# Attention of a two-layer trunk: keys' remainder and meta values on all 128 rows, one tile for the meta probabilities, 24 gate steps ahead

## The chip, the cores and the metric

The kernel runs on one core of one Trainium2 chip. The metric is the device time of one execution in microseconds (us); lower is better. The core's engines work side by side: TensorE (PE in the profile, its weight loads PEld) for matmuls and transposes, VectorE (DVE), ScalarE (ACT), GpSimd (POOL), and SyncE (SP), which issues most DMAs. Each engine takes its own instructions in one fixed order.

## The reference, cut to what matters

The whole program is a two-layer trunk over 1040 tokens (16 meta tokens in front of 1024) of width 1024. The change touches layer 0's mixer, which has a recurrent part and an attention part side by side:

```
x_rnn, gate, q, k, v = split(h @ w_in)
y_rnn = gelu(gate) * rg_lru(x_rnn)            # conv, two sigmoid gates, a scan over time
q, k  = rotary(rmsnorm(q)), rotary(rmsnorm(k))   # 8 heads on 2 kv heads, 64 wide
# query blocks of 128 tokens; each sees 16 meta keys and 256 window keys
s = concat([q @ k_meta.T, q @ k_win.T]) * 64**-0.5, masked
p = softmax(concat([s, sink]))[..., :-1]
o = p[..., :16] @ v_meta + p[..., 16:] @ v_win
h = h + concat([y_rnn, o]) @ w_out
```

Behind it come a feed-forward layer, multi-scale retention and a second feed-forward layer, whose code the change leaves as it is. All is in float32.

## The kernel before, in words

**Precision.** A float32 operand of a large product is split into a rounded part "hi" and a remainder "lo" (`part`, L108; L111 and L113), and a product is three matmuls, hi·hi, lo·hi and hi·lo (`mm3`, L160 to L162). A scheduler puts the instructions of each engine into their order when the program is built; the code's order is its priority, and its own model of durations decides the rest.

**Before attention.** `rnn_in` makes the recurrent inputs, then four recurrences `recur(m)` (L387) and three groups of q/k/v projections are interleaved: keys and values first (grp 2), then two groups of queries. A recurrence goes over all engines in turn: matmuls and sigmoids (L403, L404), exp and tanh on ScalarE (L406, L407), L410 on VectorE, a square root on ScalarE (L411), products on GpSimd, and two scans on VectorE (L419). `qk_transpose` (L515) turns keys and queries into columns. Heads of kv group g lie on rows 64g to 64g+63. For the keys it writes `kH[g]`, the rounded keys of group g, on its own 64 rows (ScalarE) and once more on the other 64 (GpSimd, L525), and the remainder into `kTl`, where each group has only its own 64 rows (L526).

**Gates.** `gate_in(m)` (L434), m from 0 to 3, is the gate's projection: three chunks of 264, 264 and 512 columns, each 24 matmuls in 4 steps of 6, a product on VectorE and a GELU. For m = 0 that is one ScalarE function; for the others `gelu_tanh` (L424) computes it with two ScalarE passes (L427, L430), three VectorE passes (L428, L431, L432) and one on GpSimd (L429). Its work tile `u` lies in the pool `bp`. That pool takes over the memory of the recurrences' pool `la` (L565, L566), so its tiles wait for the last scan of `recur(3)`; the query tiles `q0` and `q1` lie there too. 12 steps (all of gate 0) are taken ahead of attention (L568); the rest is handed to `background()`, which runs one step after each score of a head.

**Attention.** Nine query blocks (the first of 16 rows), each in two steps, one for a kv group with its four heads; 18 steps. `queries` splits the block's queries: hi on the group's own 64 rows, lo on the other 64 (L624, L625). `scores` (L628) makes for each head a pair of matmuls into one bank: L636 with all 128 rows against `kH` (hi·hi + lo·hi) and L637 with 64 rows against `kTl` (hi·lo); then a masked minimum on VectorE (L639) and an exp on ScalarE (L641). GpSimd copies the 16 meta columns of the four heads into `pm` (L645). One step later, `transposes` turns the probabilities (L653) and `pm` (L658, 64 columns) and copies them to SBUF. Two steps later, `values` multiplies the meta part by `vmb[g]`, a 64-row matrix with the meta values of the four heads in block form (L666, 256 columns), and the window part head by head (L670). `finish` transposes the result (L687). After step 13 the first half of the output projection `out_proj(m, 0)` joins the background work; `gate_out` splits the gated recurrences at steps 10 to 13.

```
for _ in range(12):
    next(gates)
...
for i in range(ns + 4):
    ...
        scores(*steps[i])
    ...
        transposes(*steps[i - 1])
    ...
        values(*steps[i - 2])
```

## Time and profile before

| | us |
|---|---|
| median of 3 runs | 2723.39 |
| lowest and highest | 2717.32, 2725.48 |
| the profiled execution | 2719.58 |
| its span, first to last instruction | 2717.5 |
| TensorE busy in the span | 2639.5 |
| VectorE busy | 1650.9 |
| GpSimd busy | 1305.2 |
| ScalarE busy | 1131.8 |

A matmul's busy time in the profile includes its way through the array, so that busy times of neighbours overlap; what a matmul costs in a stream is the distance from its start to the next one's start. "Clock" is the share of the 2.4 GHz that was granted to TensorE; 0.50 is the lower of its two levels, 1.2 GHz. A bracket at a row's end gives the engine's idle time before it and what ended it.

### The profile page before, as it was taken

The numbers are of one execution on the slowest core, as the hardware profiler recorded it, in microseconds if no ns is written. First come the engines' busy times: TensorE is split into PE (matmuls) and PEld (weight loads), VectorE is DVE, ScalarE is ACT, GpSimd is POOL, SyncE is SP. The second block draws the span as 40 slices with busy tenths as digits, with TensorE's granted clock in tenths as the row PEclk, the third lists the DMA queues.
The fourth block names the chain that finished last, engine by engine and source line by source line (L and its number), as shares of the span: only waits on it lengthen the run. The fifth ranks groups of instructions, "written<-read, shape, count | busy, mean of one in ns | idle before, by whom it ended". The sixth has DMA issues, their size and how long they took to land.

```text
span 2717.5 us, 43025 instructions
## 1 busy us (share of the span) xinstructions
PE 2639.5 (97%) x16151; PEld 2331.9 (86%) x16151; DVE 1650.9 (61%) x2976; ACT 1131.8 (42%) x2328; POOL 1305.2 (48%) x1215
## 2 busy tenths in 40 slices
PE   8979999999999899999999999999998999998999
PEld 7867899999999899888888888888886788886777
DVE  6866675866666877634434454344378555556875
ACT  4665543433333433343434444334443333334442
POOL 3654233555545777533334243342444555565784
PEclk9989999999999999999999999999999999999999
DMA  4000142232232743222121242222241232226442
GB/s 150 26 30 16 64 152 83 102 110 87 98 111 99 266 137 95 102 77 78 57 92 63 85 137 74 86 78 73 84 140 62 93 113 97 102 89 233 160 150 89
DMA packets 111073, 274.60 MB, mean 101 GB/s; under 512 B 13520, under 2 KB 13776, under 8 KB 110864
## 3 DMA queue, kind: packets, MB, share of 16 engines
q1 hardware_dynamic: 87840, 228.86, 25.1%
q10 hardware_dynamic: 22464, 41.14, 4.0%
q8 instruction: 127, 2.08, 0.3%
q0 software_dynamic: 560, 1.85, 0.2%
q14 instruction: 82, 0.67, 0.1%
HBM read 216.37 MB, written 55.43 MB: 100 GB/s over the span
## 4 chain that ended last, share of the span: by engine, by line
PE 53%; DVE 3%; POOL 1%; ACT 1%; issue 1%; DMA 0%; SPq 0%; DVEq 0%; ACTq 0%; POOLq 0%
PE ps L161 13%; PE ps L160 13%; PE ps L162 13%; PE ax L160 4%; PE ax L161 4%; PE ax L162 4%; DVE lo L113 1%; PE ax L1081 1%; PE ax L186 1%; DVE xp L760 1%; PE ax L1135 0%; POOL ol L781 0%; DVE ol L781 0%; DVE T L775 0%; PE ax L1096 0%
## 5 line engine op out<-in xcount | busy, mean ns | idle before, releaser
L160 PE MATMUL ps<-oh,hi 128*128 128x260 f32 (+1 forms) x1584 | 506.2, 322 | 19.4 <-ACT oh L780 13.8
L162 PE MATMUL ps<-oh,lo 128*128 128x260 f32 (+1 forms) x1584 | 506.7, 321 | 10.5 <-DVE lo L113 10.4
L161 PE MATMUL ps<-ol,hi 128*128 128x260 f32 (+1 forms) x1584 | 508.7, 322 | 1.1 <-DVE ol L781 1.0
L111 ACT CAST hi<-raw 128x512 fp32r<-128x512 f32 (+2 forms) x476 | 284.6, 602 | 531.4 <-PE ps L161 345.8
L160 PE MATMUL ax<-oh,hi 128*128 128x260 f32 (+1 forms) x1212 | 388.0, 322 | 2.0 <-ACT hi L111 0.8
L162 PE MATMUL ax<-oh,lo 128*128 128x260 f32 (+1 forms) x1212 | 387.0, 321 | 2.6 <-DVE lo L113 2.6
L161 PE MATMUL ax<-ol,hi 128*128 128x260 f32 (+1 forms) x1212 | 389.0, 321 | 0.4 <-DVE ol L781 0.4
L113 DVE TENSOR_TENSOR lo<-raw,hi 128x512 fp32r<-128x512 f32 (+2 forms) x348 | 282.1, 813 | 113.8 <-ACT hi L111 103.8
L113 DVE TENSOR_TENSOR lo<-S,hi 128x512 fp32r<-128x512 f32 (+2 forms) x288 | 257.3, 896 | 138.3 <-ACT hi L111 132.5
L111 ACT CAST hi<-S 128x512 fp32r<-128x512 f32 (+2 forms) x288 | 161.2, 562 | 427.8 <-PE ps L161 186.8
L160 PEld LDWEIGHTS ps<-oh,hi 128*128 128x128 f32 x1584 | 298.4, 189 | 45.9 <-ACT oh L780 15.3
L162 PEld LDWEIGHTS ps<-oh,lo 128*128 128x128 f32 x1584 | 299.1, 189 | 36.7 <-DVE lo L113 13.3
L161 PEld LDWEIGHTS ps<-ol,hi 128*128 128x128 f32 x1584 | 299.2, 189 | 26.9 <-DVE ol L781 3.2
L113 POOL TENSOR_TENSOR lo<-raw,hi 128x512 fp32r<-128x512 f32 x128 | 166.0, 1304 | 266.9 <-ACT hi L111 255.6
L160 PE MATMUL ps<-xh,hi 128*128 128x512 f32 (+1 forms) x752 | 278.7, 372 | 10.7 <-ACT hi L111 7.1
L161 PE MATMUL ps<-xl,hi 128*128 128x512 f32 (+1 forms) x752 | 275.7, 367 | 1.7 <-DVE xl L210 1.1
L162 PE MATMUL ps<-xh,lo 128*128 128x512 f32 (+1 forms) x752 | 273.2, 364 | 0.0
L291 POOL TENSOR_TENSOR t<-t,rf 128x520 f32<-128x520 f32 (+1 forms) x148 | 215.3, 1464 | 78.8 <-DVE t L822 31.7
L160 PEld LDWEIGHTS ax<-oh,hi 128*128 128x128 f32 x1212 | 229.7, 190 | 21.4 <-ACT hi L111 1.2
L162 PEld LDWEIGHTS ax<-oh,lo 128*128 128x128 f32 x1212 | 229.2, 189 | 21.4 <-DVE lo L113 3.3
L161 PEld LDWEIGHTS ax<-ol,hi 128*128 128x128 f32 x1212 | 229.6, 189 | 19.0 <-DVE ol L781 0.8
L781 POOL TENSOR_TENSOR ol<-raw,oh 128x520 fp32r<-128x520 f32 (+1 forms) x140 | 204.9, 1491 | 26.0 <-ACT oh L780 13.1
(323 smaller groups left out, 5722.3 us busy)
## 6 DMA issues: line engine op xcount, KB each, us to landing
raw<-in_wr_dram SPq DMA_DIRECT2D x64, 512.0 KB, 3.2
raw<-in_wgu_dram SPq DMA_DIRECT2D x48, 512.0 KB, 3.3
rb<-in_wgu_dram SPq DMA_DIRECT2D x40, 512.0 KB, 3.2
raw<-hd SPq DMA_DIRECT2D x77, 260.0 KB, 3.8
raw<-hd SPq DMA_DIRECT2D x77, 256.0 KB, 3.0
raw<-in_wrv_dram SPq DMA_DIRECT2D x32, 512.0 KB, 3.2
raw<-in_wro_dram SPq DMA_DIRECT2D x32, 512.0 KB, 3.2
hd<-T ACTq DMA_DIRECT2D x44, 260.0 KB, 2.6
```

Source lines behind the costliest of these rows:

```text
L111: nc.scalar.copy(hi, src)
L113: eng.tensor_tensor(out=lo, in0=src, in1=f32(hi), op=ALU.subtract)
L160: nc.tensor.matmul(ps, ah, bh, start=first and i == 0, stop=False, skip_group_check=more)
L161: nc.tensor.matmul(ps, ah, bl, start=False, stop=False, skip_group_check=more)
L162: nc.tensor.matmul(ps, al, bh, start=False, stop=last and i == n - 1, skip_group_check=more)
L186: nc.tensor.matmul(o, a, b, start=first and i == 0 and j == 0, stop=end and j == 1)
L291: (eng or nc.vector).tensor_tensor(out=out_, in0=a, in1=b, op=ALU.mult)
L760: nc.vector.scalar_tensor_tensor(out=t[:, :n], in0=h[m][hf][:, :n], scalar=par(gname, m), in1=sc, op0=ALU.mult, op1=ALU.mult)
L781: eng.tensor_tensor(out=lo, in0=src, in1=f32(hi), op=ALU.subtract)
L1081: nc.tensor.matmul(ps[:, :P], kf[d][:, c:c + P], qf[d][:, c:c + P], start=d == 0, stop=d == 1)
```

## The change

- `kTl` becomes two tiles `kL[g]` with the remainder on all 128 rows: VectorE writes the group's own 64 rows as before, and GpSimd copies them to the other 64 (18 new copies). The second matmul of a score pair then takes all 128 rows of the query tile. On the added rows the query's lo meets the key's lo, a product that was left out before.
- The meta probabilities of both kv groups share one tile `pm` of 128 columns; it is transposed once per block, and the meta values are one 128-row matrix `vmb` of 512 columns, so that a block has one such matmul instead of two. `values` runs once per block, for all eight heads, when the second group's step is due.
- 24 gate steps, gates 0 and 1, are taken ahead of attention instead of 12, and `gelu_tanh`'s work tile comes from the general pool of slots instead of `bp`.
- For room: `part` with a pool gets one buffer instead of two, the first half of a weight unit uses the common pool, and `sn` has two buffers instead of three.

```diff
         def gelu_tanh(y, x, n):
-            u = bp.tile([P, 528], F32, tag="gu", bufs=1, name=nm("gu"))[:, :n]
+            u = slot("gu")[:, :n]
             nc.scalar.activation(u, x, AF.Square)
             nc.vector.scalar_tensor_tensor(out=u, in0=u, scalar=0.044715, in1=x, op0=ALU.mult, op1=ALU.mult)
             nc.gpsimd.tensor_tensor(out=u, in0=u, in1=x, op=ALU.add)
...
                     gs = slice(g * 64, (g + 1) * 64)
                     nc.scalar.copy(kH[g][(gs,) + at], src[gs])
                     nc.gpsimd.tensor_copy(kH[g][(slice(64 - g * 64, 128 - g * 64),) + at], kH[g][(gs,) + at])
-                    nc.vector.tensor_tensor(out=kTl[(gs,) + at], in0=src[gs], in1=f32(kH[g][(gs,) + at]),
+                    nc.vector.tensor_tensor(out=kL[g][(gs,) + at], in0=src[gs], in1=f32(kH[g][(gs,) + at]),
                                             op=ALU.subtract)
+                    nc.gpsimd.tensor_copy(kL[g][(slice(64 - g * 64, 128 - g * 64),) + at], kL[g][(gs,) + at])
             else:
                 for j in range(2):
                     nc.tensor.transpose(pt[:, j * P:j * P + n], qs[:n, j * P:(j + 1) * P], ident[:n, :n])
...
         lctx.close()
         bp = bctx.enter_context(tc.tile_pool(name="bp", bufs=1))
         gates = chain.from_iterable(gate_in(m) for m in range(4))
-        for _ in range(12):
+        for _ in range(24):
             next(gates)
         work = [gates]
...
         nsk = mp.tile([P, 8], F32, name="nsk")
         nc.vector.tensor_scalar(nsk, par("sink", 0, 8), -1.0, None, op0=ALU.mult)
-        vmb = []
+        vmb = mp.tile([P, 512], F32, name="vmb")
+        nc.gpsimd.memset(vmb, 0.0)
+        ps = bank()
+        nc.tensor.matmul(ps[:, :P], c0t[:NM, C0["rep"]:C0["rep"] + P], vt[:NM, 0, :], start=True, stop=True)
         for g in range(2):
-            ps = bank()
-            nc.tensor.matmul(ps[:64, :64], c0t[:NM, C0["rep"]:C0["rep"] + 64], vt[:NM, 0, g * 64:(g + 1) * 64],
-                             start=True, stop=True)
-            v_ = mp.tile([64, 256], F32, name=f"vmb{g}")
-            mul(v_.rearrange("p (h d) -> p h d", d=64), ps[:64, :64].unsqueeze(1).to_broadcast([64, 4, 64]),
-                c0t[:64, C0["bm"]:C0["bm"] + 256].rearrange("p (h d) -> p h d", d=64))
-            vmb.append(v_)
+            gs = slice(g * 64, (g + 1) * 64)
+            mul(vmb[gs, g * 256:(g + 1) * 256].rearrange("p (h d) -> p h d", d=64),
+                ps[gs, gs].unsqueeze(1).to_broadcast([64, 4, 64]),
+                c0t[gs, C0["bm"]:C0["bm"] + 256].rearrange("p (h d) -> p h d", d=64))
         h8 = cp.tile([P, KD * 8], F32, name="h8")
         ya = [[(slot("yah", F32R), slot("yal", F32R)) for _ in range(2)] for _ in range(4)]
...
             k.mo = 128 if b >= 2 else 0
             k.den = bp.tile([P, 8], F32, tag="den", bufs=3, name=nm("den"))
             k.nmx = bp.tile([P, 8], F32, tag="nmx", bufs=3, name=nm("nmx"))
-            k.p, k.sb, k.pm, k.pmT = {}, {}, {}, {}
+            k.p, k.sb = {}, {}
+            k.pm = bp.tile([P, P], F32, tag="pm", bufs=2, name=nm("pm"))
             return k
         def queries(k):
...
         def scores(k, g):
             n, wn = k.n, k.w1 - k.w0
             wm = 272 if k.b else wn
-            gs = slice(g * 64, (g + 1) * 64)
             k.p[g] = bp.tile([P, 4, 272], F32, tag="p", bufs=3, name=nm("p"))
             for i in range(4):
                 hd = g * 4 + i
                 ps = bank("ps")
                 nc.tensor.matmul(ps[:n, :wm], k.q[g][:, i, :n], kHf[g][:, k.w0:k.w0 + wm], start=True, stop=False)
-                nc.tensor.matmul(ps[:n, :wm], k.q[g][gs, i, :n], kLf[gs, k.w0:k.w0 + wm], start=False, stop=True)
-                sn = bp.tile([P, 272], F32, tag="sn", bufs=3, name=nm("sn"))
+                nc.tensor.matmul(ps[:n, :wm], k.q[g][:, i, :n], kLf[g][:, k.w0:k.w0 + wm], start=False, stop=True)
+                sn = bp.tile([P, 272], F32, tag="sn", bufs=2, name=nm("sn"))
                 nc.vector.tensor_tensor_reduce(sn[:n, :wn], ps[:n, :wn], k.mk, -0.125, nsk[:n, hd:hd + 1],
                                                ALU.add, ALU.min, k.nmx[:n, hd:hd + 1])
                 nc.scalar.activation(k.p[g][:n, i, :wn], sn[:n, :wn], AF.Exp, bias=k.nmx[:n, hd:hd + 1], scale=-1.0,
                                      accum_out=k.den[:n, hd:hd + 1])
                 background()
-            k.pm[g] = bp.tile([P, 64], F32, tag="pm", bufs=2, name=nm("pm"))
-            nc.gpsimd.tensor_copy(k.pm[g][:n].rearrange("p (h d) -> p h d", d=NM), k.p[g][:n, :, k.mo:k.mo + NM])
+            nc.gpsimd.tensor_copy(k.pm[:n, g * 64:(g + 1) * 64].rearrange("p (h d) -> p h d", d=NM),
+                                  k.p[g][:n, :, k.mo:k.mo + NM])
         def transposes(k, g):
             n = k.n
...
                 sb = slot("pT")[:, :512]
                 (nc.scalar.copy if off else nc.vector.tensor_copy)(sb, pt)
                 k.sb[g].append(sb)
-            pt = bank()
-            nc.tensor.transpose(pt[:64, :n], k.pm[g][:n], ident[:n, :n])
-            k.pmT[g] = bp.tile([64, P], F32, tag="pmT", bufs=2, name=nm("pmT"))
-            nc.vector.tensor_copy(k.pmT[g][:, :n], pt[:64, :n])
-
-        def values(k, g):
-            n, segs = k.n, k.sb[g]
-            if g == 0:
-                k.po = bank("ps")
-            nc.tensor.matmul(k.po[:n, g * 256:(g + 1) * 256], k.pmT[g][:, :n], vmb[g], start=True, stop=not segs)
-            for i in range(4):
-                o = g * 256 + i * 64
-                for j, sb in enumerate(segs):
-                    nc.tensor.matmul(k.po[:n, o:o + 64], sb[:, i * P:(i + 1) * P],
-                                     vt[:, k.b - len(segs) + 1 + j, g * 64:(g + 1) * 64],
-                                     start=False, stop=i == 3 and j == len(segs) - 1)
             if g == 1:
...
+                pt = bank()
+                nc.tensor.transpose(pt[:, :n], k.pm[:n], ident[:n, :n])
+                k.pmT = bp.tile([P, P], F32, tag="pmT", bufs=2, name=nm("pmT"))
+                nc.vector.tensor_copy(k.pmT[:, :n], pt[:, :n])
+
+        def values(k):
+            n = k.n
+            k.po = bank("ps")
+            nc.tensor.matmul(k.po[:n], k.pmT[:, :n], vmb, start=True, stop=not k.segs)
+            for g in range(2):
+                segs = k.sb[g]
+                for i in range(4):
+                    o = g * 256 + i * 64
+                    for j, sb in enumerate(segs):
+                        nc.tensor.matmul(k.po[:n, o:o + 64], sb[:, i * P:(i + 1) * P],
+                                         vt[:, k.b - len(segs) + 1 + j, g * 64:(g + 1) * 64],
+                                         start=False, stop=g == 1 and i == 3 and j == len(segs) - 1)
...
         def finish(k):
             n, c = k.n, k.c
...
                 gate_out(i - 10)
             if 0 <= i - 1 < ns:
                 transposes(*steps[i - 1])
-            if 0 <= i - 2 < ns:
-                values(*steps[i - 2])
+            if 0 <= i - 2 < ns and steps[i - 2][1] == 1:
+                values(steps[i - 2][0])
             if 0 <= i - 4 < ns and steps[i - 4][1] == 1:
                 finish(steps[i - 4][0])
             if i == fin0:
```

The scheduler then orders the engines anew. In its rows a name is a tile's with its number; `ps` and `ax` are PSUM banks, `gt` and `gu` a gate's product and GELU work tile, `hl` the recurrence's state, `xc` and `rg` its work tiles.

On TensorE, before the change, the queries' last transposes and the two small meta-value products (L586) are followed at once by the first score pair:

```order
L530 MATMUL ax335_2222<-ckt_68,qs308_2052 128x128
L530 MATMUL ax336_2227<-ckt_68,qs313_2098 128x128
L530 MATMUL ax337_2232<-ckt_68,qs318_2144 128x128
L586 MATMUL ax348_2337<-vt_733,c0t_312 64x64
L586 MATMUL ax349_2341<-vt_733,c0t_312 64x64
L636 MATMUL ps387_2399<-kH0_730,q0384_2380 16x16
L637 MATMUL ps387_2399<-kTl_732,q0384_2380 16x16
L160 MATMUL ps396_2417<-xh14_131,hi390_2407 128x264
L161 MATMUL ps396_2417<-xl15_133,hi390_2407 128x264
```

With the change the second gate's last chunk `ps358` stands there, and the small product (now one, L587) and the first score pair come behind it:

```order
L162 MATMUL ps358_2425<-xh72_294,lo352_2362 128x512
L160 MATMUL ps358_2425<-xh75_301,hi351_2360 128x512
L161 MATMUL ps358_2425<-xl76_303,hi351_2360 128x512
L162 MATMUL ps358_2425<-xh75_301,lo352_2362 128x512
L587 MATMUL ax360_2462<-vt_734,c0t_312 128x128
L637 MATMUL ps407_2529<-kH0_730,q0404_2510 16x16
L638 MATMUL ps407_2529<-kL0_732,q0404_2510 16x16
L160 MATMUL ps416_2547<-xh14_131,hi410_2537 128x264
L161 MATMUL ps416_2547<-xl15_133,hi410_2537 128x264
```

What moved: gate 1's three chunks, 72 matmuls, stand ahead of the first score.

On VectorE, before the change, the last recurrence's two scans (L419) stand right behind L410 and the two products that make `vmb`:

```order
L291 TENSOR_TENSOR gt344_2252<-ps347_2307,R92_493 128x512
L113 TENSOR_TENSOR lo508_2926<-raw504_2918,hi507_2924 128x512
L410 SCALAR_TENSOR_TENSOR xc322_2165<-xc322_2165,rg323_2166 128x1040
L291 TENSOR_TENSOR vmb0_2339<-ax348_2337,c0t_312 64x256
L291 TENSOR_TENSOR vmb1_2343<-ax349_2341,c0t_312 64x256
L419 SCALAR_TENSOR_TENSOR hl325_2172<-av324_2167,hl325_2172 128x528
L419 SCALAR_TENSOR_TENSOR hl330_2190<-av324_2167,hl325_2172,hl330_2190 128x512
L639 ISA sn388_2402,nmx367_2363<-ps387_2399,c0t_312,nsk_2335 16x16
```

With the change, gate 1's GELU, two weight remainders of the output projection (`lo674`, `lo676`), its last gate product `gt354` and `vmb` stand between L410 and the scans:

```order
L410 SCALAR_TENSOR_TENSOR xc322_2184<-xc322_2184,rg323_2185 128x1040
L428 SCALAR_TENSOR_TENSOR gu357_2418<-gu357_2418,gt353_2364 128x528
L113 TENSOR_TENSOR lo674_3648<-raw672_3644,hi673_3646 128x512
L431 SCALAR_TENSOR_TENSOR gu357_2418<-gu357_2418,gt353_2364 128x528
L432 SCALAR_TENSOR_TENSOR hl191_1227<-gu357_2418,hl191_1227 128x528
L291 TENSOR_TENSOR gt354_2365<-ps358_2425,R92_493 128x512
L291 TENSOR_TENSOR vmb_2460<-ax360_2462,c0t_312 64x256 x2
L113 TENSOR_TENSOR lo676_3652<-raw672_3644,hi675_3650 128x512
L419 SCALAR_TENSOR_TENSOR hl325_2191<-av324_2186,hl325_2191 128x528
L428 SCALAR_TENSOR_TENSOR gu359_2451<-gu359_2451,gt354_2365 128x512
L419 SCALAR_TENSOR_TENSOR hl330_2209<-av324_2186,hl325_2191,hl330_2209 128x512
L431 SCALAR_TENSOR_TENSOR gu359_2451<-gu359_2451,gt354_2365 128x512
```

What moved: the scans come behind six more passes and behind `vmb`, which reads what L587 wrote.

On ScalarE, before the change, the square root L411 follows gate 0's GELU and its table load, and the queries' casts (L624) follow the square root:

```order
L444 ACTIVATE gt344_2252<-gt344_2252 128x512
L411 ACT_TABLE_LOAD
L411 ACTIVATE xc322_2165<-xc322_2165 128x1040
L624 CAST q0384_2380<-qT118_734 64x16
L624 CAST q0384_2380<-qT120_736 64x16
L624 CAST q0384_2380<-qT122_738 64x16
L624 CAST q0384_2380<-qT124_740 64x16
```

With the change the tanh L407 and gate 1's passes are mixed in, and a weight cast and another table load for L430's tanh follow the square root:

```order
L444 ACT_TABLE_LOAD
L444 ACTIVATE gt343_2270<-gt343_2270 128x528
L407 ACTIVATE rg323_2185<-rg323_2185,cpos_321 128x1040
L444 ACTIVATE gt344_2271<-gt344_2271 128x512
L532 COPY qT125_742<-ax337_2251 128x128
L427 ACTIVATE gu357_2418<-gt353_2364 128x528
L411 ACT_TABLE_LOAD
L411 ACTIVATE xc322_2184<-xc322_2184 128x1040
L111 CAST hi673_3646<-raw672_3644 128x512
L430 ACT_TABLE_LOAD
L430 ACTIVATE gu357_2418<-gu357_2418 128x528
L111 CAST hi675_3650<-raw672_3644 128x512
```

What moved: L407 stands behind the GELU's table load, and gate 1's passes down to L430's tanh stand where the queries' casts stood.

## Rows read from the trace of the kernel before

**Rows 1.** The page: TensorE's busy time, and the chain that ended last.
```profile
PE 2639.5 (97%) x16151; PEld 2331.9 (86%) x16151; DVE 1650.9 (61%) x2976; ACT 1131.8 (42%) x2328; POOL 1305.2 (48%) x1215
...
PE 53%; DVE 3%; POOL 1%; ACT 1%; issue 1%; DMA 0%; SPq 0%; DVEq 0%; ACTq 0%; POOLq 0%
```

**Rows 2.** All engines by stretch: length; busy PE, PEld, DVE, ACT, POOL; clock, DMA.
```profile
185.70:196.60 10.90, 0.01 (x1) 0.00 (x0) 3.62 (x5) 5.51 (x15) 6.14 (x11) 0.50 0.14 48
196.60:202.00 5.40, 5.33 (x28) 4.96 (x28) 0.58 (x5) 1.85 (x4) 4.60 (x17) 0.52 0.01 2
196.60:269.65 73.05, 72.98 (x395) 57.26 (x396) 40.96 (x133) 35.77 (x125) 37.23 (x83) 0.94 0.05 15
269.65:303.72 34.07, 34.07 (x213) 25.98 (x211) 25.22 (x79) 23.30 (x76) 13.79 (x36) 1.00 0.24 79
```

**Rows 3.** Line L637 alone by stretch: length, PE, PEld, clock, DMA.
```profile
269.65:303.72 34.07, 8.08 (x21) 3.84 (x21) 1.00 0.24 79
303.72:357.00 53.28, 5.89 (x16) 2.74 (x15) 1.00 0.13 46
```

**Rows 4.** TensorE in time order, 270 us: start, us, line, tiles, shape.
```profile
269.65 1.03 PE L653 MATMUL ax<-ckt,p 128*128 128x128 f32 x8
270.52 0.27 PE L658 MATMUL ax<-ckt,pm 128*64 128x128 f32 x1
270.63 0.27 PE L653 MATMUL ax<-ckt,p 128*128 128x128 f32 x1
270.84 0.70 PE L666 MATMUL ps<-vmb,pmT 64*128 64x256 f32 x2
271.46 2.00 PE L670 MATMUL ps<-vt,pT 128*128 128x64 f32 x16
273.27 0.37 PE L636 MATMUL ps<-kH,q 128*128 128x272 f32 x1
273.57 0.39 PE L637 MATMUL ps<-kTl,q 64*128 64x272 f32 x1
273.89 0.39 PE L636 MATMUL ps<-kH,q 128*128 128x272 f32 x1
```

**Rows 5.** TensorE in time order, 321 us, other matmuls around a pair.
```profile
320.79 0.28 PE L162 MATMUL ps<-yrh,lo 128*128 128x264 f32 x1
320.91 0.29 PE L636 MATMUL ps<-kH,q 128*128 128x272 f32 x1
321.13 0.39 PE L637 MATMUL ps<-kTl,q 64*128 64x272 f32 x1
321.45 1.77 PE L670 MATMUL ps<-vt,pT 128*128 128x64 f32 x14
```

**Rows 6.** TensorE in time order at the start of attention.
```profile
185.03 0.68 PE L586 MATMUL ax<-vt,c0t 16*64 16x64 f32 x4
196.67 0.20 PE L636 MATMUL ps<-kH,q 128*16 128x16 f32 x1 [10.96 <-POOL q L625]
```

**Rows 7.** ScalarE in time order before the start of attention.
```profile
187.74 1.28 ACT L411 ACT_TABLE_LOAD   x1
189.03 1.07 ACT L411 ACTIVATE xc<-xc 128x1040 f32<-128x1040 f32 x1
```

**Rows 8.** VectorE in time order before the start of attention.
```profile
194.06 1.28 DVE L419 TENSOR_TENSOR_SCAN hl<-av,hl,hl 128x512 f32<-128x512 f32 x1
```

**Rows 9.** TensorE in time order, a gate chunk of 512 columns.
```profile
208.36 0.39 PE L160 MATMUL ps<-xh,hi 128*128 128x512 f32 x1
208.59 0.39 PE L161 MATMUL ps<-xl,hi 128*128 128x512 f32 x1
```

**Rows 10.** Groups by line, 196 to 356 us: busy, mean ns, idle before.
```profile
L431 DVE SCALAR_TENSOR_TENSOR gu<-gu,gt 128x528 f32<-128x528 f32 x3 | 2.3, 783 | 0.0
```

**Rows 11.** Line L525: count, ns min/median/max, first and last start.
```profile
L525 POOL CAST kH<-kH x18: 285/348/1933, 86.5 to 122.7; 64x128 fp32r<-64x128 f32 x18
```

**Rows 12.** All engines, 86 to 126 us, columns as in rows 2.
```profile
86.00:126.00 40.00, 33.88 (x259) 30.98 (x259) 36.38 (x120) 25.80 (x60) 25.28 (x35) 1.00 0.08 27
```

More of the change, by code (lines that the diff above doesn't have):

```diff
@@ L56 @@
 _o = 0
-for _n, _w in (("mask", 272), ("cos", 72), ("sin", 72), ("rep", 64), ("bm", 256)):
+for _n, _w in (("mask", 272), ("cos", 72), ("sin", 72), ("rep", 128), ("bm", 256)):
     C0[_n] = _o
@@ L108, in part @@
     def part(src, w, eng=nc.vector, pool=None):
-        hi = (pool or stg).tile([P, 512], F32R, tag="hi", bufs=2 if pool else 6, name=nm("hi"))[:, :w]
+        hi = (pool or stg).tile([P, 512], F32R, tag="hi", bufs=1 if pool else 6, name=nm("hi"))[:, :w]
         nc.scalar.copy(hi, src)
-        lo = (pool or stg).tile([P, 512], F32R, tag="lo", bufs=2 if pool else 6, name=nm("lo"))[:, :w]
+        lo = (pool or stg).tile([P, 512], F32R, tag="lo", bufs=1 if pool else 6, name=nm("lo"))[:, :w]
         eng.tensor_tensor(out=lo, in0=src, in1=f32(hi), op=ALU.subtract)
@@ L122, in unit @@
             nc.sync.dma_start(raw, src)
-            return [part(raw[:, i * 512:(i + 1) * 512], 512, eng, pool) for i in range(2)]
+            return [part(raw[:, i * 512:(i + 1) * 512], 512, eng, pool if i else None) for i in range(2)]
     def unit4(src):
@@ L480, in tile_hybrid @@
         kH = [mp.tile([P, 8, 144], F32R, name=f"kH{g}") for g in range(2)]
-        kTl = mp.tile([P, 8, 144], F32R, name="kTl")
+        kL = [mp.tile([P, 8, 144], F32R, name=f"kL{g}") for g in range(2)]
         kHf = [t.rearrange("p b c -> p (b c)") for t in kH]
-        kLf = kTl.rearrange("p b c -> p (b c)")
+        kLf = [t.rearrange("p b c -> p (b c)") for t in kL]
         vt = mp.tile([P, 9, P], F32, name="vt")
@@ new lines, in transposes @@
+            if g == 1:
+                pt = bank()
[14 more added lines that the diff above has]
+                                         start=False, stop=g == 1 and i == 3 and j == len(segs) - 1)
+            es = bp.tile([P, 8], F32, tag="es", bufs=2, name=nm("es"))
+            nc.vector.tensor_tensor(out=es[:n], in0=k.nmx[:n], in1=nsk[:n], op=ALU.subtract)
+            nc.scalar.activation(es[:n], es[:n], AF.Exp)
+            nc.vector.tensor_tensor(out=k.den[:n], in0=k.den[:n], in1=es[:n], op=ALU.add)
+            nc.vector.reciprocal(k.den[:n], k.den[:n])
+            k.yt = slot("yt")[:, :512]
+            mul(k.yt[:n].rearrange("p (h d) -> p h d", d=64), k.po[:n].rearrange("p (h d) -> p h d", d=64),
+                k.den[:n].unsqueeze(2).to_broadcast([n, 8, 64]))
@@ L1276, in _constants @@
         c0[:n, C0["sin"] + 8 * b:C0["sin"] + 8 * b + 8] = as_[t0:t0 + n]
-    for h in range(4):
+    for h in range(8):
         for k in range(NM):
             c0[k, C0["rep"] + h * NM + k] = 1.0
-        c0[h * NM:(h + 1) * NM, C0["bm"] + h * 64:C0["bm"] + (h + 1) * 64] = 1.0
+        c0[h * NM:(h + 1) * NM, C0["bm"] + h % 4 * 64:C0["bm"] + (h % 4 + 1) * 64] = 1.0
     rc, rs = table(256, 10000.0)
```

8 lines of the change are left out of this document (removed).

## The prediction, made before the changed kernel ran

> **What bounds the kernel now.** I read the page first. TensorE is busy 97% of the span, and more than half of the chain that ended last is its own; no other engine has over 3% of that chain, and no queue has 1% [rows 1]. So a change pays here if it takes time from TensorE's stream or closes a hole in it, and work on another engine costs nothing until TensorE waits for it.
>
> Next I read all engines by stretch around attention [rows 2]. From the first score (196.60 us) to 269.65 TensorE is busy 72.98 of 73.05 us, and in the 34.07 us behind that, until the first output-projection matmul, all of it. In between VectorE has 25.22 and ScalarE 23.30 of 34.07 us: not far behind. Two losses show. The first is the hole ahead of attention: TensorE does 0.01 us of work between 185.70 and 196.60. The clock there is 0.50, and 0.52 in the 5.4 us of work behind it. What ends the hole is the first query split on GpSimd, L625 [rows 6]. Query tiles lie in `bp`, which takes over the memory of the recurrence, so L625 can't run before the last scan, which ends at 194.06 + 1.28 = 195.34 [rows 8]; the score starts 1.33 us later.
>
> The second loss is inside the stream, and the time line shows it at the 64-row matmuls. Around a score pair among output-projection matmuls [rows 5] the 264-column L162 takes 0.12 from its start to the next one's, L636 0.22 and the 64-row L637 0.32. A 272-column matmul among full-row neighbours would take the 0.12, so the pair costs 0.54 where 0.24 would do: 0.30 too much, 0.10 on the way into the 64 rows and 0.20 out of them. Where pairs follow each other, L636 takes 0.30 and L637 0.32 [rows 4], 0.38 too much. L666, also on 64 rows, shows the same entry: the transpose ahead of it takes 0.21 (270.63 to 270.84) where the eight at 269.65 took 0.11 each.
>
> **The change part by part.**
>
> *Widened matmuls.* Of 72 pairs 64 are full and 8 belong to the 16-row block. At 0.30 to 0.38 the full ones give 19.2 to 24.3; I take 0.34, between the two, so 21.8. For a 16-column pair no row shows the step; it lies between nothing and 0.34, 0 to 2.7 in all, and I take the middle, 1.4. The 18 L666 give their entry of 0.10 for certain, 1.8; if they leave at L637's 0.20, 5.4, which I take because the entry is the same. Their columns stay: 18 of 256 become 9 of 512. Nine transposes L658 fewer at 0.11 are 1.0. Sum 29.6, with bounds of 22.0 and 33.4. This is TensorE's time and counts as long as TensorE sets the pace.
>
> The rule that speaks against it is in the Trainium skill, "TensorE: Matmul & The Clock Gate", "Why this matters for your kernels": a single matmul with 32 rows takes the same time as one with 128. By it the widening would save nothing, and rival C below holds. The same skill's "TensorEngine Tiling (Array Packing)", "Key Properties", says that a change of tiling mode drains TensorE, which is what [rows 4, 5] look like; by that the sum stays.
>
> *Twelve more gate steps ahead.* Gate 1 is 48 matmuls of 264 columns at 0.12 and 24 of 512 at 0.23 [rows 9], 11.3 us. They leave attention's stream and go where TensorE idles: that alone would give 11.3. But the scans slip. Before, the square root ends at 189.03 + 1.07 = 190.10 [rows 7], and the scans end 5.2 later. Now behind the square root ScalarE has a 512-column cast, a table load and the tanh: 0.53 + 1.28 + 0.53 = 2.3, the load from the same rows, the passes at half of the 1040-column one. Then VectorE has five passes of a gate or a remainder at 0.78 [rows 10], 3.9, the two half-wide `vmb` products, 0.8, and two scans of 1.28, 2.6: together 9.6 instead of 5.2, so 4.4 later. The square root itself comes later too, as the tanh L407 ahead of it now stands behind the GELU's table load, another 1.3 or so. Behind the scans wait the `bp` tiles: the query split, and so the first score. I take a slip of 6 us, so the first score starts near 202.5 and the part gains 11.3 - 6 = 5.3. If the passes hide behind the square root's own wait the slip is 0; if gate 0's and gate 1's GELUs queue up it can eat all of the 11.3. Bounds: a gain of 0 to 11.3. The hole stays some 10 us long, since gate 1's matmuls fill its old place only until about 191.5.
>
> *The second copy of the remainder.* 18 copies like the 18 of L525, median 0.35 [rows 11], are 6.3 us of GpSimd work between 86 and 127 us. GpSimd idles 14.7 of the 40 us there [rows 12], which hides it; VectorE has 3.6 idle, so a delay can pass on to it. I charge 1, and 5 as the bound without that cover (most of the 6.3).
>
> *A longer stretch without filler.* One background step runs per score. Before, 36 gate steps are left at the first score, so they last 9 of 18 steps; then comes the stretch from 269.65, with 21 scores [rows 3] and no gate matmuls, until the output projection starts after step 13. Now 24 are left and last 6 steps, while the output projection's place stays: 8 steps, 32 scores, run bare. In them TensorE for 21 scores takes 34.07 less 21 x 0.34, less 1.6 for five L666 and 0.3 for transposes: 25.1, so 38.2 for 32. VectorE at 25.22 for 21 needs 38.4 for 32, ScalarE 35.5 [rows 2]. Three engines come out even, each score goes through all three in turn, and `sn` has two buffers where it had three: TensorE will wait there, with no gate matmul to put in. Nothing is lost if the engines interlock perfectly; I charge 6 us, and 15 as the bound, a little above the 13.7 of rival B.
>
> *The rest at nothing.* `gu` from a slot, one buffer for `part` with a pool, and one copy `pmT` fewer per block: no queue holds 1% of the chain [rows 1], and the output projection whose weights use these buffers starts behind the bare stretch, with ScalarE and GpSimd both under 70% busy in the stretch before it [rows 2]. Without that cover a late weight part would add to the 6 us above.
>
> *Sum.* -29.6 - 5.3 + 1 + 6 = -27.9. The profiled execution took 2719.58 and the median is 2723.39, 3.8 above; so about 2692 for such an execution, and 2695.5 for a median. All good ends together (-33.4 - 11.3) give 2679, all bad ones (-22.0 + 5 + 15 = -2.0) 2721.
>
> **The rivals.**
>
> *A, as forecast:* 2680 to 2703. Chance 0.66.
>
> *B, the bare stretch keeps its old pace.* Not TensorE but the round from score to minimum to exp to the next free buffer sets the pace, still 34.07 / 21 = 1.62 us per score or a little more. 32 scores then take 51.9 instead of 38.2, so +13.7 in place of +6, and 2703; at 1.9 us each, 2712. For it: VectorE's and ScalarE's sums equal TensorE's, and a buffer less. Against it: before, TensorE was never idle in that stretch, so no such round showed. Chance 0.22, a fifth of that near enough to no change.
>
> *C, the rows don't matter.* The 0.3 per pair belongs to two matmuls into one bank, or to the q and k tiles, whatever their row count. Then 29.6 falls to the 1.0 of the transposes, and -1.0 - 5.3 + 1, with none to 6 us of waits, is -5.3 to +0.7: 2718 to 2724, no change. Against it: gate matmuls follow each other into one bank at 0.23 for 512 columns [rows 9], and the transpose ahead of L666 pays 0.10 with another bank and another tile. This is where the rule on 32 rows from the page "TensorE: Matmul & The Clock Gate" would lead. Chance 0.04.
>
> *D, the other side: the clock falls in the bare stretch.* TensorE, waiting a little at every score, gets the lower level there (0.50, 1.2 GHz) as it does in and behind the hole [rows 2]. 38.2 us of its work would take up to 76.4. 28 us of that work at the lower level cancel the gain, over 36 make the kernel slower by more than 0.3%; the whole stretch gives 2734. For it: in rows 2 the clock was still 0.52 for 5.4 us of work after 10.9 idle. Against it: the same stretch was granted 1.00 before, and the waits that I charge are short. Chance 0.08, nearly all of it slower.
>
> **How the numbers follow.** The forecast is A's, 2695.5. The spread of this kernel's runs is about 0.3%, some 8 us, and that is also what I count as a change: under 2715 faster, over 2732 slower. A's own range is 2680 to 2703. Half of B lies above that, and C and D lie above 2715, so the range of 8 in 10 goes to 2714 at the upper end. Faster: A and four fifths of B, 0.84. Same: the rest of B, C and a little of D, 0.09. Slower: D, 0.07.
>
> **What would show it.** Widening: pairs at 0.12 and 0.12 among other matmuls, and no step of 0.2 ahead of the block's `vmb` product. Gate 1: the distance between the small product L587 and the first score, and the time of that score, 202.5; if it is 208, this part is worth nothing. The bare stretch: the time from the last gate matmul to the first output-projection matmul, 38 to 44, with idle time of TensorE on `nmx`, `sn` or a free bank; that first matmul should come some 21 us earlier than at 303.72 (48 pairs of the 64 and most of the rest, 22.7, and 5.3, less 7). Copies: GpSimd's share between 86 and 126, and where the queries' work starts. The prediction is wrong if pairs keep their 0.3, if the granted clock falls in the bare stretch, or if TensorE's idle time there passes 15 us.

## The result, and the profile after

The changed kernel took 2690.72 us (median of 4 runs, 2688.25 to 2692.26) against 2722.09 us before (now also 4 runs); the ratio is 0.9885, 95% interval 0.9867 to 0.9903. The forecast was 2695.5. The profiled execution took 2692.10, 27.5 less than the one of before. Of gates only, one of the kernels below, four of twelve executions took 2749.66 to 2753.70 us at a granted clock of 0.973 to 0.975 (0.988 to 0.992 in the other eight), and its ratio leaves out three of the four.

The page first: TensorE's busy time, and the chain that ended last.

```profile
PE 2614.7 (97%) x16122; PEld 2328.5 (87%) x16122; DVE 1648.6 (61%) x2967; ACT 1130.2 (42%) x2328; POOL 1324.9 (49%) x1234
...
PE 88%; DVE 6%; ACT 3%; issue 1%; POOL 1%; DMA 1%; SPq 0%; ACTq 0%; DVEq 0%; POOLq 0%
```

TensorE is still busy 97% of the span, with 24.8 us less work than in [rows 1]. Next a pair among output-projection matmuls in TensorE's time line (lines 2 and 3 are the pair; L638 is the old L637):

```profile
297.07 0.28 PE L162 MATMUL ps<-yrh,lo 128*128 128x264 f32 x1
297.19 0.29 PE L637 MATMUL ps<-kH,q 128*128 128x272 f32 x1
297.32 0.29 PE L638 MATMUL ps<-kL,q 128*128 128x272 f32 x1
297.44 0.28 PE L160 MATMUL ps<-yrh,hi 128*128 128x264 f32 x1
```

Every step is 0.12 to 0.13, where [rows 5] had 0.22 and 0.32. The start of attention, in TensorE's time line:

```profile
193.62 0.48 PE L587 MATMUL ax<-vt,c0t 16*128 16x128 f32 x2
207.26 0.19 PE L637 MATMUL ps<-kH,q 128*16 128x16 f32 x1 [13.16 <-POOL q L627]
```

The hole is longer than in [rows 6], 13.16 us, and the first score comes 10.59 us later. All engines by stretch (columns as in rows 2): the hole, then to the last gate matmul, then to the first output-projection matmul:

```profile
193.70:207.20 13.50, 0.41 (x2) 0.21 (x2) 9.39 (x12) 6.18 (x15) 8.46 (x11) 0.59 0.11 39
207.26:240.55 33.29, 33.17 (x208) 29.42 (x208) 20.75 (x73) 19.21 (x71) 25.38 (x56) 0.91 0.05 17
240.55:286.79 46.24, 42.98 (x315) 36.63 (x314) 39.29 (x133) 35.17 (x127) 26.11 (x65) 1.00 0.19 59
```

The output projection starts 16.9 us earlier than before (286.79 for 303.72; the forecast was some 21). In the stretch without filler TensorE idles 3.26 us and VectorE works 39.29 of 46.24. To see what attention as a whole gained, take the stretch from the first score to the last transposes of its output (L687, now L689), of before and of the changed kernel:

```profile
196.67:368.25 171.58, 171.58 (x1076) 140.61 (x1077) 103.76 (x315) 85.87 (x275) 61.17 (x132) 0.98 0.14 47
```

```profile
207.26:342.63 135.37, 131.99 (x977) 120.45 (x978) 95.07 (x296) 79.36 (x267) 59.14 (x130) 0.98 0.17 56
```

Attention ends 25.6 us earlier. The remaining 1.9 us came behind it, in code that the change doesn't touch.

### The profile page after: what moved, and what is told of

The parts are those of the page before. It is cut to its first block, busy times and chain, and to the rows that moved or that the text cites. A ratio compares the mean times of both kernels' runs of the same rounds, so it can differ in the third digit from the quotient of the medians.

```text
span 2690.0 us, 42990 instructions
## 1 busy us (share of the span) xinstructions
PE 2614.7 (97%) x16122; PEld 2328.5 (87%) x16122; DVE 1648.6 (61%) x2967; ACT 1130.2 (42%) x2328; POOL 1324.9 (49%) x1234
## 4 chain that ended last, share of the span: by engine, by line
PE 88%; DVE 6%; ACT 3%; issue 1%; POOL 1%; DMA 1%; SPq 0%; ACTq 0%; DVEq 0%; POOLq 0%
PE ps L160 20%; PE ps L161 20%; PE ps L162 20%; PE ax L160 8%; PE ax L161 8%; PE ax L162 8%; DVE lo L113 1%; PE ps L673 1%; POOL ol L783 1%; DVE ol L783 1%; PE ax L1083 1%; DVE xp L762 1%; PE ax L186 1%; DVE T L777 0%; ACT hi L111 0%
## 5 line engine op out<-in xcount | busy, mean ns | idle before, releaser
L160 PE MATMUL ps<-oh,hi 128*128 128x260 f32 (+1 forms) x1584 | 509.0, 324 | 20.0 <-ACT oh L782 11.6
L162 PE MATMUL ps<-oh,lo 128*128 128x260 f32 (+1 forms) x1584 | 508.3, 322 | 8.7 <-DVE lo L113 8.6
L162 PE MATMUL ax<-oh,lo 128*128 128x260 f32 (+1 forms) x1212 | 387.4, 322 | 2.6 <-DVE lo L113 2.6
L162 PEld LDWEIGHTS ps<-oh,lo 128*128 128x128 f32 x1584 | 300.3, 190 | 34.6 <-DVE lo L113 10.8
L162 PE MATMUL ps<-xh,lo 128*128 128x512 f32 (+1 forms) x752 | 273.1, 364 | 0.0
L162 PEld LDWEIGHTS ax<-oh,lo 128*128 128x128 f32 x1212 | 229.4, 189 | 21.6 <-DVE lo L113 3.6
```

Of the source, the lines that this page charges most:

```text
L160: nc.tensor.matmul(ps, ah, bh, start=first and i == 0, stop=False, skip_group_check=more)
L162: nc.tensor.matmul(ps, al, bh, start=False, stop=last and i == n - 1, skip_group_check=more)
```

## The experiments

"Attention" below is the stretch just shown; "idle" is its length less TensorE's busy time in it. Ratios are to the kernel before on the same chip.

| kernel | median | ratio (95%) | first score | attention | idle | attention ends |
|---|---|---|---|---|---|---|
| before | 2722.09 | | 196.67 | 171.58 | 0.0 | 368.25 |
| changed | 2690.72 | 0.9885 (0.9867 to 0.9903) | 207.26 | 135.37 | 3.4 | 342.63 |
| scores only, 12 steps | 2689.58 | 0.9890 (0.9865 to 0.9915) | 196.53 | 146.72 | 0.3 | 343.25 |
| gates only | 2718.82 | 0.9994 (0.9961 to 1.0026) | 209.64 | 157.42 | 0.0 | 367.06 |
| both widenings, 12 steps | 2692.28 | 0.9895 (0.9871 to 0.9920) | 196.67 | 145.04 | 3.1 | 341.71 |
| late GELU | 2695.85 | 0.9910 (0.9883 to 0.9937) | 203.56 | 137.25 | 5.6 | 340.81 |
| recurrences early | 2687.65 | 0.9887 (0.9874 to 0.9901) | 199.83 | 133.23 | 3.6 | 333.06 |
| recurrences early, 12 steps | 2680.21 | 0.9856 (0.9843 to 0.9870) | 182.73 | 147.47 | 4.7 | 330.20 |
| filler spread | 2690.62 | 0.9896 (0.9882 to 0.9909) | 207.69 | 134.06 | 3.1 | 341.75 |
| `sn` in slots | 2700.87 | 0.9936 (0.9922 to 0.9949) | 208.29 | 142.55 | 6.2 | 350.84 |
| early, 12 steps, split divided | 2682.38 | 0.9862 (0.9848 to 0.9876) | 188.32 | 143.10 | 2.4 | 331.42 |
| both on 64 rows | 2705.18 | 0.9949 (0.9936 to 0.9961) | 196.16 | 163.85 | 0.0 | 360.01 |
| split divided | 2690.41 | 0.9888 (0.9872 to 0.9903) | 207.43 | 139.30 | 2.0 | 346.73 |
| changed, again | 2695.57 | 0.9908 (0.9894 to 0.9922) | 208.53 | 135.52 | 3.4 | 344.05 |

What lies behind attention took 2344.1 to 2354.6 us in these profiled executions (span less the last column), and 2347.4 and 2344.2 in the two of the changed kernel itself. So parts of a few us are read from the stretches, not from the totals.

### Which part gains: each part alone

Scores only (from the changed kernel, with the meta code of before):

```diff
-        for _ in range(24):
+        for _ in range(12):
...
-        vmb = mp.tile([P, 512], F32, name="vmb")
+        vmb = []
...
-            if 0 <= i - 2 < ns and steps[i - 2][1] == 1:
-                values(steps[i - 2][0])
+            if 0 <= i - 2 < ns:
+                values(*steps[i - 2])
```

> The changed kernel with 12 gate steps ahead and with the two-part meta probabilities of before: only the scores' second matmul is widened (its smaller buffers stay). Theory (a 64-row matmul costs its stream 0.3 to 0.4 us in the step into it and out of it): the first score stays near 197 us, a pair among other matmuls steps by 0.12 and 0.12, the widening saves 23 less a wait of about 2 us, so 2700 us, 0.992 of before. Rival (the row count costs nothing, what was gained comes from the other two parts): 2722, ratio 1.000, pairs keep 0.5 to 0.6.

Gates only (24 steps; narrow scores and the meta code of before):

```diff
-                nc.tensor.matmul(ps[:n, :wm], k.q[g][:, i, :n], kLf[g][:, k.w0:k.w0 + wm], start=False, stop=True)
+                nc.tensor.matmul(ps[:n, :wm], k.q[g][gs, i, :n], kLf[g][gs, k.w0:k.w0 + wm], start=False, stop=True)
...
-                    nc.gpsimd.tensor_copy(kL[g][(slice(64 - g * 64, 128 - g * 64),) + at], kL[g][(gs,) + at])
```

> The changed kernel with 64-row second matmuls (no second copy of the remainder) and with the two-part meta probabilities: only the 24 gate steps ahead and the smaller buffers stay. Theory (gate 1's GELU ahead of the last scans delays attention by as much as its matmuls save): first score near 207 us, 11.3 us of matmuls gone from attention's stream, so 2721 us, within 3 of before, with TensorE hardly idle in the stretch without filler, since its 1.6 us per score covers the other engines. Rival 1 (my forecast's term): 2717. Rival 2 (24 steps are worth their full 11 us): 2711.

Both widenings with 12 steps (the first edit of the first diff alone):

> The changed kernel with 12 gate steps ahead instead of 24; both widenings stay. Theory: the hole ahead of attention is 11 us again and the first score near 197, gate 1's matmuls return to attention's stream, the stretch without filler is shorter; 2690 to 2693, as the changed kernel. Rival (24 steps are worth the 5.3 of the forecast): 2696. Rival (24 steps are a loss, through waits in the stretch without filler): 2686.

Attention's stretch of the three, in that order, each a view of its own kernel:

```profile
196.53:343.25 146.72, 146.47 (x1076) 132.78 (x1077) 102.35 (x315) 84.90 (x275) 65.19 (x132) 0.98 0.17 55
```

```profile
209.64:367.06 157.42, 157.42 (x1005) 128.21 (x1005) 96.68 (x305) 80.34 (x267) 59.67 (x130) 0.99 0.15 48
```

```profile
196.67:341.71 145.04, 141.98 (x1049) 130.25 (x1050) 102.72 (x306) 84.97 (x275) 62.52 (x132) 0.98 0.17 56
```

The widened scores alone give the whole gain: 2689.58, and 25.1 us less TensorE work (171.58 - 146.47), 0.39 for each of the 64 full pairs. The ratio is 0.989 where I expected 0.992; attention is 24.9 us shorter where I expected 21. Rival C's claim is out: gates only has the remainder in two tiles as well, but narrow matmuls, and its L637 is busy for a mean of 388 ns as in the kernel before, against 288 in scores only. The gates alone give next to nothing, as expected: the first score comes 13.0 later, the stretch is 14.2 shorter. The meta matrix takes 4.5 us of work away (146.47 - 141.98), and 2.8 of them come back as idle time. Both widenings with 12 steps took the 2690 to 2693 expected of them.

Part of these differences is TensorE's clock. Attention in the kernel before has 8.5 us at 0.50: 5.1 right behind the hole, and 3.4 among gate matmuls, with TensorE busy all through the 10 us ahead:

```profile
232.70:242.70 10.00, 10.00 (x51) 7.34 (x50) 7.12 (x17) 4.62 (x13) 4.39 (x8) 1.00 0.13 44
242.71:246.12 3.41, 3.41 (x18) 3.41 (x18) 0.25 (x4) 0.77 (x4) 1.96 (x4) 0.50 0.08 30
```

Scores only has 4.4 us at 0.50, gates only 3.4 and both widenings 5.1, all behind the hole. If half of such time is lost, an estimate, then 2.0 of the 25.1 us, 2.6 of the 14.2 and 1.7 of what both widenings save need not be the edits' own. A full pair would then give 0.36.

### What a narrow matmul costs: the change of rows, or the narrowness

In the kernel before, the first matmul of a pair goes on 64 rows as well:

```diff
-                nc.tensor.matmul(ps[:n, :wm], k.q[g][:, i, :n], kHf[g][:, k.w0:k.w0 + wm], start=True, stop=False)
+                nc.tensor.matmul(ps[:n, :wm], k.q[g][gs, i, :n], kHf[g][gs, k.w0:k.w0 + wm], start=True, stop=False)
```

> The kernel before, with the first matmul of each score pair on the group's own 64 rows too, so that the product of the queries' remainder with the rounded keys is left out. Theory (what costs is the change between 128 and 64 rows, once on the way in and once on the way out): a pair still changes twice, so attention takes as long as before, 2718 within 3 us, and the step inside a pair is 0.12. Rival (a 64-row matmul is itself 0.2 to 0.3 us slower than one of 128 rows): 13 to 19 us longer, 2731 to 2737, and both steps of a pair are near 0.3.

TensorE's time line of the kernel before, a pair among gate matmuls and the start of two pairs that follow each other:

```profile
211.38 0.39 PE L161 MATMUL ps<-xl,hi 128*128 128x512 f32 x1
211.61 0.29 PE L636 MATMUL ps<-kH,q 128*128 128x272 f32 x1
211.83 0.39 PE L637 MATMUL ps<-kTl,q 64*128 64x272 f32 x1
212.15 0.50 PE L162 MATMUL ps<-xh,lo 128*128 128x512 f32 x1
212.49 0.29 PE L636 MATMUL ps<-kH,q 128*128 128x272 f32 x1
```

TensorE's time line of the experiment, a single pair, then two in a row:

```profile
316.87 0.28 PE L161 MATMUL ps<-yal,hi 128*128 128x264 f32 x1
317.08 0.39 PE L636 MATMUL ps<-kH,q 64*128 64x272 f32 x1
317.31 0.28 PE L637 MATMUL ps<-kTl,q 64*128 64x272 f32 x1
317.53 0.39 PE L162 MATMUL ps<-yah,lo 128*128 128x264 f32 x1
317.75 0.29 PE L160 MATMUL ps<-yah,hi 128*128 128x264 f32 x1
```

```profile
262.62 0.39 PE L636 MATMUL ps<-kH,q 64*128 64x272 f32 x1
262.84 0.29 PE L637 MATMUL ps<-kTl,q 64*128 64x272 f32 x1
262.97 0.29 PE L636 MATMUL ps<-kH,q 64*128 64x272 f32 x1
263.10 0.29 PE L637 MATMUL ps<-kTl,q 64*128 64x272 f32 x1
263.31 0.50 PE L160 MATMUL ps<-xh,hi 128*128 128x512 f32 x1
263.65 0.39 PE L161 MATMUL ps<-xl,hi 128*128 128x512 f32 x1
```

The rival fell: twice as many narrow matmuls make attention 7.7 us shorter. My theory missed too, as it had attention as long as before and 2718 us, where 2705.18 were measured (of the 13.4 us that the profiled span lost, 5.2 lie behind attention). A single pair costs the same as before: 0.88 from 316.87 to 317.75 for four steps of 0.12, so 0.40 too much, against 0.10 + 0.20 + 0.11 before (the last is L162 at 212.15, which takes 0.34 where 512 columns need 0.23). Each change of the row count adds about 0.1 to each of two neighbouring steps. My expectation that the step inside a pair would be 0.12 was wrong for single pairs (0.22 to 0.23); it is 0.13 between narrow neighbours at 262.84 and 262.97, where [rows 4] had 0.30 and 0.32. Pairs that follow each other now share their changes. In this trace there are eight runs of two full pairs and one of three, so 10 shared changes, some 4 of the 7.7 us at 0.40 each. By the estimate above another 2.3 are the clock's (4.0 us at 0.50 here, 8.5 before); the remaining 1.4 were not traced.

The rule of 32 rows in the Trainium skill ("TensorE: Matmul & The Clock Gate", "Why this matters for your kernels") agrees, carried over to these 64 rows, with the steps between narrow neighbours, but not with the cost beside wide ones. The drain at a change of tiling mode in the Trainium skill ("TensorEngine Tiling (Array Packing)", "Key Properties") fits these rows, which put a price on the change; that the engine drains there is not shown by them.

### Why the gates ahead gain nothing

Gate 1's GELU behind the first scores:

```diff
+                    elif m == 1:
+                        late.append((hl[m][hf][:, :b], ts[hf][:, :b], b))
...
                 scores(*steps[i])
+            if i in (0, 1):
+                gelu_tanh(*late[i])
```

> The changed kernel with gate 1's two GELUs issued behind the first two steps' scores instead of ahead of attention; its matmuls stay ahead. Theory (the GELU's passes and its table load stand between the last recurrence's square root and its scans): scans end near 199 instead of 204.5, first score near 200.5 instead of 207.3, 2684 to 2686 us. Rival (the slip comes from the matmuls ahead of the recurrence's, so the square root is what is late): first score still at 205 or later, 2689 to 2692.

The first score came at 203.56, between the two theories: the GELU's passes are worth 3.7 of the 10.6 us, the rest of the slip stays, and the square root ends at 195.16, not earlier than in the changed kernel (194.46). Attention ends 1.8 us earlier than in the changed kernel, but idles 5.6 us, and the total of 2695.85 is above both expectations.

What delays the rest shows in the changed kernel's rows: ScalarE around the square root, VectorE's second scan, and GpSimd behind it.

```profile
191.43 0.65 ACT L427 ACTIVATE gu<-gt 128x528 f32<-128x528 f32 x1
192.09 1.28 ACT L411 ACT_TABLE_LOAD   x1
193.39 1.07 ACT L411 ACTIVATE xc<-xc 128x1040 f32<-128x1040 f32 x1
```

```profile
203.18 1.28 DVE L419 TENSOR_TENSOR_SCAN hl<-av,hl,hl 128x512 f32<-128x512 f32 x1
```

```profile
203.34 2.17 POOL L429 TENSOR_TENSOR gu<-gu,gt 128x512 f32<-128x512 f32 x1 [4.49 <-DVE gu L428]
205.57 0.85 POOL L626 CAST q<-qT 64x16 fp32r<-64x16 f32 x5
```

The square root ends at 194.46, 4.36 later than in [rows 7]. The scans end 10.00 behind it (5.24 before) and the first score 2.80 behind the scans (1.33 before), since GpSimd's L429 stands ahead of the query casts. The 4.36 come from TensorE: line L403, the recurrences' own matmuls (count, ns, first and last start), in the 12-step kernel with both widenings and in the changed one:

```profile
L403 PE MATMUL ax<-xc,wa x24: 383/386/592, 64.7 to 179.1; 128*128 128x264 f32 x16, 128*128 128x512 f32 x8
```

```profile
L403 PE MATMUL ax<-xc,wa x24: 383/386/593, 65.9 to 182.9; 128*128 128x264 f32 x16, 128*128 128x512 f32 x8
```

The last one starts 3.8 us later, because gate matmuls stand among them; the Square L427 (0.65) stands ahead of the square root's table load. With the late GELU, which has no L427 there, the distance from the last L403 to the end of the square root is the same 11.0 us (184.2 to 195.16) as with 12 steps (179.1 to 190.10); in the changed kernel it is 11.6. So the slip of 10.59 adds up: 4.36 to the square root, 4.76 more to the scans, 1.47 more to the score.

If the wait for the last scans makes the hole, it must go when the recurrences come earlier:

```diff
         recur(0, xs[0])
+        recur(1, xs[1])
...
-            m = (1, 2, 3)[(2, 0, 1).index(grp)]
-            recur(m, xs[m])
+            if grp != 1:
+                m = 2 if grp == 2 else 3
+                recur(m, xs[m])
```

> The changed kernel with each recurrence one place earlier: recur(1) ahead of the first projection group, recur(2) behind it, recur(3) behind the second group instead of the third. Theory (the hole ahead of attention is the wait for the last recurrence's scans, whose memory the query tiles take): TensorE has no hole of 13 us there, the first score follows the last gate matmul within some 3 us, and unless the projections slow down by the earlier recurrences the time is 8 to 10 us under the changed kernel: 2681. Rival (the hole is only moved: VectorE, busy over 90% during the projections, makes TensorE wait there instead): the hole is gone but the first score is still near 205, 2689 to 2692.

> As the run before it, but with 12 gate steps ahead. Theory: with no hole left to fill, the number of gate steps ahead hardly matters; the same 2681 within 3 us, with less waiting in the stretch without filler (under 1.5 us instead of 3.4). Rival (the gates ahead are what keeps TensorE busy while the queries' last steps run): 5 to 10 us slower than with 24.

TensorE's time line of the first of the two, at the start of attention:

```profile
199.42 0.48 PE L589 MATMUL ax<-vt,c0t 16*128 16x128 f32 x2
199.83 0.18 PE L639 MATMUL ps<-kH,q 128*16 128x16 f32 x1
199.87 0.17 PE L640 MATMUL ps<-kL,q 128*16 128x16 f32 x1
```

The hole is gone in both. With 24 steps attention ends 9.6 us earlier than in the changed kernel, but the median is only about 3 lower and the ratio no better (0.9887), where I expected 8 to 10; what lies behind attention took 2351.3 us in the profiled execution, 4.0 more than in the changed kernel's. With 12 steps it ends 12.4 earlier and the time is 2680.21, as expected. The idle time of 4.7 us was not (under 1.5 expected). An expectation below gives it as 4.0, counted from 186.69; the first score comes at 182.73:

```profile
182.73 0.17 PE L639 MATMUL ps<-kH,q 128*16 128x16 f32 x1
```

### What TensorE waits for where there is no filler

A background step behind every second score:

```diff
-                background()
+                if i % 2 == 0 or k.b >= 7:
+                    background()
```

> The changed kernel with its 24 remaining gate steps spread over the first 14 attention steps: one behind every second score instead of every one. Theory (TensorE's 3.4 us of idle time in attention arise where no filler is left): that idle time falls under 1 us, the last transposes of attention come 2 to 3 us earlier, 2688. Rival (the waits belong to the new order of the block's values, not to the missing filler): idle time stays over 2.5 us, no gain.

`sn` in a slot:

```diff
-                sn = bp.tile([P, 272], F32, tag="sn", bufs=2, name=nm("sn"))
+                sn = slot("sn")[:, :272]
```

> The changed kernel with the score tile sn in a slot of the large pool, so that its two buffers no longer limit anything. Theory (the waits in the stretch without filler are those of the round through VectorE and ScalarE, not of the buffers): TensorE's idle time in attention stays at 2.5 to 3.5 us, 2690. Rival (two buffers instead of three are the cause): idle time under 1.5 us, 2688.

Spreading changed nothing (idle 3.1, where I expected under 1), so the missing filler isn't the whole cause. With `sn` in slots the waits grew to 6.2 and the time to 2700.87, outside both expectations. That doesn't clear the two buffers by itself, as its longest wait (2.49 us, ahead of the score pair at 249.63) is one that the changed kernel hasn't. But scores only has two buffers as well and idles 0.3, so they alone aren't the cause. And the clock fell. All engines by stretch in that kernel:

```profile
262.00:272.30 10.30, 8.49 (x69) 7.54 (x68) 6.67 (x21) 8.49 (x30) 6.18 (x15) 1.00 0.00 2
272.30:286.00 13.70, 13.39 (x56) 12.36 (x57) 7.46 (x28) 5.61 (x21) 3.68 (x8) 0.50 0.49 157
```

TensorE waited 1.8 us in the 10.3 us ahead, and then ran 13.70 us at 0.50, the lower level (1.2 GHz). That is rival D, on a smaller scale: the stretch without filler takes 53.76 us instead of 46.24.

In the changed kernel's time line of TensorE 1.6 of 2.7 us of waits sit at steps 10 to 13, where ScalarE's casts of the gated recurrences (`gate_out`) stand among the exps; the other 1.1 come from 247 to 249 us, ahead of these casts. The half of the time axis that isn't needed yet is split later:

```diff
             if 10 <= i < 14:
-                gate_out(i - 10)
+                gate_out(i - 10, (0,))
+            if 14 <= i < 18:
+                gate_out(i - 14, (1,))
```

> The kernel with earlier recurrences and 12 gate steps ahead, and with the split of the gated recurrences divided: the first halves of the time axis at steps 10 to 13, the second halves at steps 14 to 17, where the output projection's matmuls fill TensorE (they aren't needed sooner). Theory (the waits of the stretch without filler come from these casts standing ahead of the exps on ScalarE): TensorE's idle time between the first score and attention's last transposes falls from 4.0 to under 2.5 us, 2678. Rival (they come from the block's values being made at once, whatever ScalarE does beside it): idle time stays near 4, 2680.

> The changed kernel with that same division of the gated recurrences' split alone. Theory: TensorE's idle time inside attention falls from 3.4 to under 2 us and the last transposes come 1 to 2 us earlier; total 2689. Rival: idle time stays over 3 us.

> The changed kernel itself, unaltered, beside the others on one chip: 2688 to 2693 us, so that the version with earlier recurrences and 12 gate steps is 8 to 12 us under it.

Idle time fell to the expected 2.4 on the early kernel, from 4.7, but its time didn't fall (2682.38). On the changed kernel it fell from 3.4 to 2.0, just short of "under 2", and attention ended 4.1 later, not earlier. The next two views show why: the changed kernel by stretch, then this one, over the same times.

```profile
240.55:250.30 9.75, 8.56 (x58) 6.81 (x57) 9.28 (x30) 6.62 (x25) 6.72 (x14) 1.00 0.16 54
250.30:264.00 13.70, 13.67 (x111) 12.60 (x110) 9.82 (x39) 10.37 (x39) 8.16 (x24) 1.00 0.22 64
```

```profile
240.44:250.30 9.86, 8.67 (x58) 6.80 (x57) 9.38 (x31) 6.75 (x26) 6.83 (x14) 1.00 0.53 168
250.30:264.00 13.70, 13.70 (x63) 13.14 (x62) 6.26 (x22) 5.93 (x23) 4.76 (x14) 0.50 0.24 74
```

With the same 58 matmuls and 1.2 us of waits ahead, the clock stayed at 1.00 in the one and went to 0.50 in the other, where 63 matmuls fit into the 13.70 us instead of 111. The execution with the fall is the slowest of its four (2686.66 to 2699.57), so the 4.1 us hold for it alone; with half of the 13.7 us taken off, an estimate, its attention would end 2.7 earlier than the changed kernel's. The changed kernel again took 2695.57, above the expected 2688 to 2693. The early version with 12 steps and divided split, on the same chip, is 13 us under it (8 to 12 expected); without the division it took 2680.21 on another chip. Either beats both kernels of this study.

## Why the prediction was right, step by step

**Widened matmuls: the size held, its parts didn't.** I summed 29.6; TensorE's work in attention fell by 171.58 - 141.98 = 29.6 at equal gate steps, some 1.7 of it by the clock. The pairs gave 25.1, some 2.0 of it by the clock, where I had 21.8 + 1.4 = 23.2: for a single pair I counted the steps into and out of the narrow matmul (0.30) and missed the one behind it, another 0.11. That the whole came out at 29.6 is luck in part. The meta part gave 4.5 where I had 5.4 + 1.0.

**Gate steps ahead: the term that failed.** I predicted a gain of 5.3 from a slip of 6. The slip was 10.59, and against the 12-step kernel with both widenings TensorE's work in attention is 9.99 less: nothing. My chain behind the square root was right (9.6 forecast, 10.00 measured). Wrong was "another 1.3 or so" for the square root itself, which came 4.36 later, as gate 1's matmuls stand among L403's on TensorE; I had followed ScalarE's order there, not TensorE's. L407 behind the GELU's table load cost nothing: it stands there in the 12-step kernel with both widenings too, whose square root ends at 190.10 as before. And I left out L429 on GpSimd ahead of the query casts, 1.47.

**Second copies: hidden.** GpSimd's busy time from 86 to 126 us rose from 25.28 [rows 12] to the 34.06 of this row of the changed kernel:

```profile
86.00:126.00 40.00, 36.30 (x269) 33.66 (x269) 37.93 (x130) 26.39 (x62) 34.06 (x51) 0.96 0.08 28
```

Yet in the 12-step kernel with both widenings the first score stands at 196.67, where it stood before. The price was nothing, not 1.

**The stretch without filler.** VectorE needed 39.29 us (38.4 forecast) and ScalarE 35.17 (35.5). TensorE's work was 42.98, not 38.2, for 33 scores instead of 32 (one score is some 1.2 of the 4.8 more; where the rest comes from was not followed), and it waited 3.26 us, not 6: 46.24 against the 44.2 of the forecast. Rival B, which puts 51.9 there, didn't come.

**Sum.** -29.6, + 10.59 - 9.99, + 3.4 of waits is -25.6, which is attention's end (368.25 to 342.63); 1.9 more came behind it. I was 4.8 us above the measured median: against the profiled execution the sum of -27.9 is 0.4 off, as 5.9 lost on the gates, 3.6 gained on waits and copies and the 1.9 behind attention nearly cancel. That closeness is luck; the medians differ by 31.4 where the two profiled executions differ by 27.5.

**Rivals.** C is refuted by the scores alone. D didn't happen in the changed kernel's two profiled executions, but did in four of its variants and not for the whole stretch: for 13.7 us with `sn` in slots and with the split divided, for 3.4 with the filler spread (from 277.76) and with the recurrences early and 12 steps (from 255.96). So its price was too high and its place was right. Waits aren't needed for such a fall: the kernel before had one of 3.4 us with TensorE busy throughout, which my rows 2 hid in a mean of 0.94. What decides whether the clock falls there stays open: the waits ahead were the same in the pair of views above. Also open is why the meta part's order makes idle time: dividing the split took off 1.3 to 2.3 us, and the rest wasn't tried.

## What to carry to other kernels

A matmul on fewer rows than its neighbours (here 64 among 128) pays at the change, on both sides and in the step behind it; fill its rows, or put narrow ones next to each other. Work moved into an idle stretch of one engine still goes ahead of something on every engine that it uses: before counting its gain, follow what it stands in front of on all of them, up to the event that ends the idle stretch. Moving that event (here the last recurrence, one group earlier) ended attention some 10 us earlier, which filling the hole didn't; the time followed clearly only with 12 gate steps ahead (0.9856 against 0.9895).

## What the hardware showed that I had not expected

A single narrow matmul of 272 columns costs its stream 0.40 to 0.41 us, more than three times the 0.12 that it takes itself, and two narrow pairs in a row pay this once. The granted clock fell to 0.50 for 13.7 us after waits that left it at 1.00 in another execution of nearly the same program, and for 3.4 us with no wait at all ahead. And the 2350 us behind attention, whose code none of these edits touches, differed by up to 10 us between kernels and by 3 us between two executions of one.
